# Two-bank PSUM copies and a first store in four DMAs, in a batched matrix product

## The chip, the cores and the metric

The kernel runs on one core of a Trainium2 chip. The metric is the device time of one execution in microseconds (us). Each kernel is executed several times, in rounds that alternate with the kernel before on the same chip, and most executions of a kernel agree within 0.3%. The span of the profile is about 2 us shorter than the time: it begins at the first instruction that the profiler shows. Executions over 1.5% above a kernel's fastest are called slow and are not used in ratios.

## The reference

```python
batch, m, k, n = 16, 512, 768, 1024
x: float32 (batch, k, m)      y: float32 (batch, k, n)
out = np.einsum('bkm,bkn->bmn', x, y)          # float32 (batch, m, n)
```

Inputs are 16 x 768 x (512 + 1,024) x 4 B = 75.5 MB, the output is 16 x 512 x 1,024 x 4 B = 33.55 MB. All of it has to cross the core's 16 DMA engines once.

## The kernel before

Each batch loads x and y in float32, casts them to bf16 on VectorE (DVE), multiplies on TensorE (PE) into PSUM, copies each 128x512 result to SBUF on ScalarE (ACT), and stores the whole 2 MB result in one DMA, four batches later. All DMAs are issued by one queue (SP), in program order.

```python
x_v = x.rearrange("b (p ko) m -> b p ko m", ko=KT)     # 12 KB contiguous per partition
y_v = y.rearrange("b (p ko) n -> b p ko n", ko=KT)     # 24 KB
o_v = out.rearrange("b (p mo) n -> b p mo n", mo=MT)   # 16 KB, MT = 4 blocks of 4 KB
...
psum = ctx.enter_context(tc.tile_pool(name="psum", bufs=8, space=bass.MemoryType.PSUM))
LAG = 4

def store(b):
    nc.sync.dma_start(o_v[b], o_tiles.pop(b)[:])

for b in range(B):
    ...
    load(xs[:], x_v[b], 1)                       # xs, ys: two buffers each
    ... load(ys[:, ks], y_v[b, :, ks], 1)        # one DMA; two halves for the last batch
    if b >= LAG:
        store(b - LAG)
    ... casts x_sb <- xs (one), y_sb <- ys (two halves)
    for h in range(halves):                      # 1, or 2 for the last batch
        for mo in range(MT):
            for nt in range(NT):                 # NT = 2, NF = 512
                if h == 0:
                    ps[mo, nt] = psum.tile([P, NF], FP32, name="ps")
                for kt in ...:
                    mm(ps[mo, nt], x_w, y_sb, kt, mo, nt)
                if h == halves - 1:
                    nc.scalar.copy(o_sb[:, mo, nt * NF:(nt + 1) * NF], ps[mo, nt][:])
for b in sorted(o_tiles):
    store(b)
```

## Time and profile before

| | before |
|---|---|
| time, median of the first 3 runs | 262.4 us (262.04 to 262.52) |
| span of the profiled execution | 260.5 us |
| DMA engines' time in packets of the one queue | 98.4% of the span |
| bytes | 109.06 MB in 49 DMAs |
| PE / DVE / ACT busy | 73% / 32% / 29% |

### The profile page before, as it was taken

The page shows a single profiled execution, that of the slowest core. Times are in us where ns is not written, and L with a number is a line of the kernel's source. Part 1 is how long each engine was busy: PE and PEld are TensorE (multiplying, and loading weights), DVE is VectorE, ACT ScalarE, POOL GpSimd, SP SyncE. Part 2 cuts the span into 40 slices and gives each one's busy share as a digit, 9 for nine tenths or more (in the row PEclk, how much of TensorE's full clock was granted, in tenths as well). Part 3 has the DMA queues.
Part 4 walks back from the last instruction along what each step waited for, and adds up shares of the span by engine and source line. Part 5 has one row for each costly group of instructions (what it writes and reads, how often), then busy time and mean ns, then how long its engine had stood idle before and what let it go on. Part 6 is the DMA issues. An engine that isn't in the chain of part 4 may idle for free.

```text
span 260.5 us, 1879 instructions
## 1 busy us (share of the span) xinstructions
PE 191.3 (73%) x768; PEld 89.3 (34%) x768; DVE 83.1 (32%) x48; ACT 76.4 (29%) x129; POOL 0.2 (0%) x4
## 2 busy tenths in 40 slices
PE   0049999897939959688496966969789395899600
PEld 0014555453513514334142432434335142355200
DVE  0271633525222252322524214252132522252000
ACT  1003444442421403324032330323314043141600
POOL 0000000000000000000000000000000000000000
PEclk9999999999985977979898896797979889799955
DMA  7999999999999999999999999999999999999994
GB/s 279 434 434 411 445 423 436 426 387 420 446 416 442 423 422 455 409 440 418 438 435 415 453 418 431 423 428 449 410 443 421 426 445 407 431 430 430 435 428 201
DMA packets 7065, 109.18 MB, mean 419 GB/s; under 512 B 784, under 2 KB 784, under 8 KB 784
## 3 DMA queue, kind: packets, MB, share of 16 engines
q1 hardware_dynamic: 7056, 109.06, 98.4%
q8 instruction: 6, 0.10, 0.1%
q14 instruction: 3, 0.02, 0.0%
HBM read 75.50 MB, written 33.55 MB: 419 GB/s over the span
## 4 chain that ended last, share of the span: by engine, by line
DMA 74%; DVE 11%; PE 8%; issue 0%; ACT 0%; SPq 0%; DVEq 0%
DMA ys<-in_y_dram 74%; DVE y_sb L78 11%; PE ps L56 8%; ACT o_sb L93 0%; SPq L50 0%; DVEq L78 0%
## 5 line engine op out<-in xcount | busy, mean ns | idle before, releaser
L56 PE MATMUL ps<-y_sb,x_sb 128*128 128x512 bf16 x768 | 191.3, 412 | 53.8 <-DVE y_sb L78 53.8
L56 PEld LDWEIGHTS <-x_sb 128*128 128x128 bf16 x768 | 89.3, 118 | 155.2 <-issue 45.9
L93 ACT COPY o_sb<-ps 128x512 f32<-128x512 f32 x128 | 75.1, 587 | 168.6 <-PE ps L56 168.2
L78 DVE CAST y_sb<-ys 128x3072 bf16<-128x3072 f32 x32 | 55.0, 1757 | 87.4 <-DMA ys<-in_y_dram 87.4
L75 DVE CAST x_sb<-xs 128x3072 bf16<-128x3072 f32 x16 | 28.2, 1760 | 66.6 <-DMA xs<-in_x_dram 60.4
L93 ACT ACT_TABLE_LOAD x1 | 1.3, 1283 | 0.7 <-PEq L110 0.7
L110 POOL MEMSET const-bfloat16-1.0<- 128x1 bf16 x1 | 0.1, 101 | 0.0
L110 POOL MEMSET const-uint8-127<- 128x1 uint8 x1 | 0.1, 101 | 0.0
L110 POOL MEMSET const-float32-0.0<- 128x1 f32 x1 | 0.1, 98 | 0.2 <-issue 0.2
L110 POOL MEMSET const-float32-1.0<- 128x1 f32 x1 | 0.1, 98 | 0.0
## 6 DMA issues: line engine op xcount, KB each, us to landing
ys<-in_y_dram SPq DMA_DIRECT2D x15, 3072.0 KB, 28.1
out_dram<-o_sb SPq DMA_DIRECT2D x16, 2048.0 KB, 32.6
xs<-in_x_dram SPq DMA_DIRECT2D x16, 1536.0 KB, 29.7
ys<-in_y_dram SPq DMA_DIRECT2D x2, 1536.0 KB, 26.1
```

Of the source, the lines that this page charges most:

```text
L56: nc.tensor.matmul(ps[:], x_w[:, kt, mo], y_sb[:, kt, nt * NF:(nt + 1) * NF], start=(kt == 0), stop=(kt == KT - 1))
L75: nc.vector.tensor_copy(x_sb[:], xs[:])
L78: nc.vector.tensor_copy(y_sb[:, ks], ys[:, ks])
L93: nc.scalar.copy(o_sb[:, mo, nt * NF:(nt + 1) * NF], ps[mo, nt][:])
L110: nc = _bacc.Bacc("TRN2", target_bir_lowering=False, num_devices=1)
```

## The change

The intent: fewer and longer copies out of PSUM (a copy takes two of the kernel's eight 128x512 result tiles at once; such a tile is called a bank here), which saves the fixed part of half of them, and a first store in pieces that could leave one by one. The diff, cut to its core (the helpers for loads and matmuls are also written out in place, with no effect on the program):

```diff
-    psum = ctx.enter_context(tc.tile_pool(name="psum", bufs=8, space=bass.MemoryType.PSUM))
+    psum = ctx.enter_context(tc.tile_pool(name="psum", bufs=4, space=bass.MemoryType.PSUM))
...
     def store(b):
-        nc.sync.dma_start(o_v[b], o_tiles.pop(b)[:])
+        o_sb = o_tiles.pop(b)
+        if b == 0:
+            for mo in range(MT):
+                nc.sync.dma_start(o_v[b, :, mo], o_sb[:, mo])
+            return
+        nc.sync.dma_start(o_v[b], o_sb[:])
...
+                    if h == 0:
+                        ps[mo] = psum.tile([P, NT, NF], FP32, name="ps")
                     for nt in range(NT):
-                        if h == 0:
-                            ps[mo, nt] = psum.tile([P, NF], FP32, name="ps")
...
-                        if h == halves - 1:
-                            nc.scalar.copy(o_sb[:, mo, nt * NF:(nt + 1) * NF], ps[mo, nt][:])
+                    if h == halves - 1:
+                        nc.scalar.copy(o_sb[:, mo].rearrange("p (t f) -> p t f", f=NF), ps[mo][:])
```

More of the change, by code (lines that the diff above doesn't have):

```diff
@@ L47 @@
     o_tiles = {}
-    def load(dst, src, rows):
-        nc.sync.dma_start(dst, src)
     def store(b):
-        nc.sync.dma_start(o_v[b], o_tiles.pop(b)[:])
-    def mm(ps, x_w, y_sb, kt, mo, nt):
-        nc.tensor.matmul(ps[:], x_w[:, kt, mo], y_sb[:, kt, nt * NF:(nt + 1) * NF],
-                         start=(kt == 0), stop=(kt == KT - 1))
+        o_sb = o_tiles.pop(b)
[4 more added lines that the diff above has]
+        nc.sync.dma_start(o_v[b], o_sb[:])
     with tc.manual_schedule():
@@ L64 @@
             halves = 2 if b == B - 1 else 1
-            load(xs[:], x_v[b], 1)
+            nc.sync.dma_start(xs[:], x_v[b])
             for h in range(halves):
                 ks = slice(h * KT // halves, (h + 1) * KT // halves)
-                load(ys[:, ks], y_v[b, :, ks], 1)
+                nc.sync.dma_start(ys[:, ks], y_v[b, :, ks])
             if b >= LAG:
@@ L86 @@
                 for mo in range(MT):
+                    if h == 0:
+                        ps[mo] = psum.tile([P, NT, NF], FP32, name="ps")
                     for nt in range(NT):
-                        if h == 0:
-                            ps[mo, nt] = psum.tile([P, NF], FP32, name="ps")
                         for kt in range(h * KT // halves, (h + 1) * KT // halves):
-                            mm(ps[mo, nt], x_w, y_sb, kt, mo, nt)
-                        if h == halves - 1:
-                            nc.scalar.copy(o_sb[:, mo, nt * NF:(nt + 1) * NF], ps[mo, nt][:])
+                            nc.tensor.matmul(
+                                ps[mo][:, nt], x_w[:, kt, mo],
+                                y_sb[:, kt, nt * NF:(nt + 1) * NF],
+                                start=(kt == 0), stop=(kt == KT - 1))
+                    if h == halves - 1:
+                        nc.scalar.copy(o_sb[:, mo].rearrange("p (t f) -> p t f", f=NF), ps[mo][:])
         for b in sorted(o_tiles):
```

## The prediction

> **What bounds the kernel now.** I read four views in this order: the page's busy shares and slices, the DMA queue totals, the stretches of time with each engine's work, and the DMA queue's own timeline. The page first:
>
> ```profile
> PE 191.3 (73%) x768; PEld 89.3 (34%) x768; DVE 83.1 (32%) x48; ACT 76.4 (29%) x129; POOL 0.2 (0%) x4
> ...
> DMA  7999999999999999999999999999999999999994
> GB/s 279 434 434 411 445 423 436 426 387 420 446 416 442 423 422 455 409 440 418 438 435 415 453 418 431 423 428 449 410 443 421 426 445 407 431 430 430 435 428 201
> ...
> q1 hardware_dynamic: 7056, 109.06, 98.4%
> ...
> HBM read 75.50 MB, written 33.55 MB: 419 GB/s over the span
> ...
> L56 PE MATMUL ps<-y_sb,x_sb 128*128 128x512 bf16 x768 | 191.3, 412 | 53.8 <-DVE y_sb L78 53.8
> ...
> L93 ACT COPY o_sb<-ps 128x512 f32<-128x512 f32 x128 | 75.1, 587 | 168.6 <-PE ps L56 168.2
> ```
>
> The reader is to see that no compute engine is above 73%, while the 16 DMA engines are busy 90% or more in 38 of 40 slices and queue q1's packets fill 98.4% of the engines' time. The bytes are the reference's: 75.5 MB of x and y in, 33.55 MB of output out, nothing read twice. Of the span of 260.5 us, the trace's packet records put the first data packet at 1.7 us and the last end at 259.3 us: 257.5 us from first to last, in which the packets fill 256.4 us per engine (98.4% of 260.5). Only about 1 us per engine is a gap. So the time is the sum of the packets' durations, plus about 3 us at the two ends.
>
> The chain of waits gives 74% to the y loads, 11% to the casts of y and 8% to matmuls. That is not three bounds in turn: a load waits for the cast that frees its buffer, but it is issued into a queue that is still long. The stretches show this best at the end (columns: PE, PEld, DVE, ACT, POOL busy us with counts; granted clock, DMA share, GB/s):
>
> ```profile
> 240.00:248.00 8.00, 5.03 (x24) 2.39 (x22) 0.00 (x0) 4.69 (x8) 0.00 (x0) 0.97 1.02 436
> 248.00:256.00 8.00, 0.00 (x0) 0.00 (x0) 0.00 (x0) 0.00 (x0) 0.00 (x0) 0.50 0.99 424
> 256.00:260.50 4.50, 0.00 (x0) 0.00 (x0) 0.00 (x0) 0.00 (x0) 0.00 (x0) 0.50 0.24 102
> ```
>
> All computing is over before 248 us, and the transfers still run at full share for another 8 us. The last store was issued at 245.7 us (chain: the last copy starts at 245.07 and takes 0.58) and its packets begin only at 252.2 us: it stood about 6.5 us behind older stores. **That 6.5 us is the slack** of the copy path at its most exposed point.
>
> **What the Trainium skill says.** (1) "DMA: Bandwidth & Descriptors", section "Where 436 GB/s comes from", gives 435 GB/s as the ceiling of the 16 ports and 425 as measured on large transfers. The trace agrees: while packets run, 109.06 MB in 256.0 us of data packets per engine is 426 GB/s, so there is about 2% to gain below the ceiling and no more. (2) The same page, "Why small descriptors are slow (HBM only)", says that each packet carries a fixed overhead of about 3 cycles. The trace shows a fixed part too, and I use its own size: median packets of 12,288, 16,384 and 24,576 B take 460, 611 and 912 ns, which is 0.0368 ns per byte plus 8 ns per packet. (3) "ScalarE: Activation LUTs", section "What ACT_TABLE_LOAD costs", gives 186 + 0.833 N ns for an instruction with immediate operands: 612 for N = 512, against 587 in this trace, so a little high here. (4) The DMA page's "Latency and other measured facts" reports that rows at a pitch of a large power of two can halve the rate, for pitches of 512 KiB and more; no row of this trace shows it, and the new store's pitch is 16 KiB.
>
> **The change, part by part.**
>
> PSUM copies. 128 copies of 512 columns become 64 of 1,024. With the page's slope, one takes 587 + 0.833 x 512 = 1,014 ns (estimate), so ACT is busy 64 x 1.014 = 64.9 us instead of 75.1: 10.2 us saved on an engine that is busy 29% and waits for PE in 168 us. Nothing of it is on the path. The copy of a pair's first half now waits for the second half's 6 matmuls, but PE keeps four pairs, the same 8 banks, and a pair comes round after 4 pairs of matmuls; the copy of 1.0 us is much shorter than three pairs' matmuls (36 x at least 0.216 = 7.8 us; where PE runs at full clock the timeline has a copy of 0.59 us and then 0.71 us of waiting for each 6 matmuls, 1.30 / 6 = 0.216), so PE should not wait for ACT. In the last batch each pair has 6 matmuls left in its second half, 6 x 0.216 = 1.3 us, more than 1.0, so copies keep up and the last ends 1.014 - 0.587 = 0.43 us later. Against 6.5 us of slack: 0 us on the end.
>
> First store. One DMA of 128 rows of 16 KB becomes four of 128 rows of 4 KB. Data packets go from 49 x 128 = 6,272 to 52 x 128 = 6,656, and completion packets (4 B, 9 ns) from 49 x 16 = 784 to 832, in all 7,056 to 7,488. A 4,096 B packet should take 8 + 4,096 x 0.0368 = 159 ns; four take 636 against 611, 25 ns more. Each engine carries 8 of the 128 rows: 8 x 25 = 200 ns, plus 3 x 9 = 27 ns. **Sum: +0.23 us**, and since the queue is the bound this is all on the path.
>
> Issue and waits. The store is issued by SP, in order with the loads:
>
> ```profile
> 31.72 0.33 SPq L50 DMA_DIRECT2D xs<-in_x_dram  x1
> 39.94 0.33 SPq L50 DMA_DIRECT2D ys<-in_y_dram  x1
> 40.32 0.42 SPq L53 DMA_DIRECT2D out_dram<-o_sb  x1
> 43.05 0.33 SPq L50 DMA_DIRECT2D xs<-in_x_dram  x1
> 52.01 0.33 SPq L50 DMA_DIRECT2D ys<-in_y_dram  x1
> 52.39 0.42 SPq L53 DMA_DIRECT2D out_dram<-o_sb  x1
> 54.05 0.33 SPq L50 DMA_DIRECT2D xs<-in_x_dram  x1
> 64.24 0.33 SPq L50 DMA_DIRECT2D ys<-in_y_dram  x1
> ```
>
> The first store's issue at 40.32 becomes four, 4 x about 0.46 = 1.9 us, done at 42.2, before the next load at 43.05 is released. The built program shows one more thing that the diff does not: a DMA may only be issued when the one eight before it, on the same of 8 completion semaphores, has landed. Three more DMAs shift this rotation. The x load of batch 6, issued at 54.05, now shares its semaphore with the y load of batch 4, which lands at 60.7 (chain of waits). So that issue moves from 54.05 to about 60.8, a **new wait of 6.7 us**. The queue then holds, behind that y load, the first store, x and y of batch 5 and the second store: 2.1 + 1.57 + 3.15 + 2.1 = 8.9 MB, at 426 GB/s some 21 us. The late load still enters 20 us before its turn, so 0 us. From batch 8 on the pairs of the rotation are as before.
>
> Sum: +0.2 us on 262.4 gives **262.6 us**.
>
> **Rivals.** (a) *The 4 KB rows at a 16 KB pitch are slow in HBM.* If 2.1 MB ran at half rate, the first store would take 9.8 us instead of 4.9: +4.9 us, about 267.3, just under 2% slower. For it speaks only point (4), at pitches 32 times larger; against it, the 16 KB rows too start at equal offsets on all engines and run at 26.8 GB/s per engine. I give it 5% in any strength. (b) *The late x load empties the queue.* It would be so if the backlog at 54 us were short; loads of y take a median of 28.1 us from issue to landing while their own bytes need 7.4, so some 20 us of backlog is the rule. If I have it wrong by all of the 6.7 us: 269. I give 1%. (c) *The copy was holding PE and a faster ACT frees it*, so that casts and loads come earlier. PE waits in the list of waits only for casts of y (53.8 us), never for ACT, and earlier loads only lengthen the queue: 262.4. (d) *Smaller packets fill the gaps between engines or smooth the shared ports.* There is about 1 us of gap in all, and one store of 16 can touch a small part of it: -0.3 us at best.
>
> **Range and chances.** The three runs before spread over 0.5 us. With +0.2 from the packets, and another execution's spread of about 0.3% either way, the range is 261.7 to 263.8, wider above because (a) and (b) only lengthen. A gain of 2% would need 5.2 us, which the bytes do not allow: 1%. A loss of 2% needs (a) or (b) near full strength: 1.5%. The rest, 97.5%, is within 2%.
>
> **What would show each step.** The page of the changed kernel should have q1 at 7,488 packets, 109.06 MB and about 98.4%; "under 8 KB" rising by 512 + 48 = 560 to 1,344; 64 ACT copies of 128x1024 at about 1,014 ns and ACT near 66 us busy; the list of waits still without a wait of PE for ACT; four store issues from 40.3 to about 42.2 us and an x load at about 60.8 in place of 54.05; the y load's period (112.06 to 127.86 in the queue's timeline, 15.8 us) unchanged; the last store issued at about 246 and landing about 13.5 us later. Wrong would be: 4,096 B packets far above 159 ns (then a is right), DMA slices below 9 between 60 and 80 us (then b), or a gap in the transfers near 246 us (then the slack was not there).

## The result, and the profile after

| | before | after |
|---|---|---|
| time, median of 4 runs each | 262.25 us (262.04 to 262.52) | 262.74 us (262.61 to 262.90) |
| ratio | | 1.0017, 95% interval 1.0002 to 1.0032 |
| span of the profiled execution | 260.5 us | 260.8 us |

A ratio is the mean time of one kernel's fast runs over that of the other's fast runs of the same rounds, so it is not quite the ratio of the medians. Here it is +0.45 us (0.0017 x 262.25): within 2%, slower by a hair.

The page of the changed kernel; its lines answer to the first fence of the prediction:

```profile
PE 191.2 (73%) x768; PEld 89.4 (34%) x768; DVE 83.1 (32%) x48; ACT 66.2 (25%) x65; POOL 0.2 (0%) x4
...
DMA  7999999999999999999999999999999999999994
GB/s 279 434 434 418 452 419 432 422 364 425 432 420 441 420 428 435 422 437 427 428 443 415 445 412 438 432 425 439 425 435 422 424 444 418 425 438 427 427 435 206
...
q1 hardware_dynamic: 7488, 109.06, 98.5%
...
L93 ACT COPY o_sb<-ps 128x1024 f32<-128x1024 f32 x64 | 64.9, 1014 | 179.2 <-PE ps L88 179.2
```

ACT has lost 10.2 us of work, exactly its 64 copies of 1,014 ns against 128 of 587, and has gained about as much waiting (179.2 us for PE instead of 168.2). The DMA row is as full as before. The largest difference in the GB/s row is its ninth value, 364 against 387 (the sixteenth, 435 against 455, is nearly as large, so one value proves little): that slice (52 to 59 us) holds the end of the y load of batch 4 and the beginning of the first store.

The queue's timeline of the changed kernel (start, duration, then the DMA and how many are merged in the line):

```profile
39.98 0.33 SPq L67 DMA_DIRECT2D ys<-in_y_dram  x1
40.36 1.85 SPq L54 DMA_DIRECT2D out_dram<-o_sb  x4
42.77 0.34 SPq L64 DMA_DIRECT2D xs<-in_x_dram  x1
51.74 0.34 SPq L67 DMA_DIRECT2D ys<-in_y_dram  x1
52.17 0.38 SPq L57 DMA_DIRECT2D out_dram<-o_sb  x1
60.56 0.33 SPq L64 DMA_DIRECT2D xs<-in_x_dram  x1
64.05 0.33 SPq L67 DMA_DIRECT2D ys<-in_y_dram  x1
```

The four issues end at 42.2 us and the next load goes out in time, at 42.77. The x load of batch 6 goes out at 60.56 instead of 54.05. In the list of the queue's waits this is a line of its own (waiter, what it waited for, us in total, times, longest). The kernel before issues all loads from one line and cannot show it, but the list of run e3 below, which has the store whole and its loads on lines of their own, has no such line:

```profile
SPq L64 <- DMA ys<-in_y_dram: 7.9, 1, 7.9
```

The end, in stretches, with the same columns as in the prediction:

```profile
240.00:248.00 8.00, 5.08 (x24) 2.45 (x22) 0.00 (x0) 4.05 (x4) 0.00 (x0) 0.96 1.00 426
248.00:256.00 8.00, 0.00 (x0) 0.00 (x0) 0.00 (x0) 0.00 (x0) 0.00 (x0) 0.50 1.02 436
256.00:260.80 4.80, 0.00 (x0) 0.00 (x0) 0.00 (x0) 0.00 (x0) 0.00 (x0) 0.50 0.29 123
```

As before, no compute engine works after 248 us while the transfers run on.

### The profile page after: what moved, and what is told of

Same layout as the page of the kernel before. It is cut to its first block, busy times and chain, and to the rows that moved or that the text cites. A ratio compares the mean times of both kernels' runs of the same rounds, so it can differ in the third digit from the quotient of the medians.

```text
span 260.8 us, 1822 instructions
## 1 busy us (share of the span) xinstructions
PE 191.2 (73%) x768; PEld 89.4 (34%) x768; DVE 83.1 (32%) x48; ACT 66.2 (25%) x65; POOL 0.2 (0%) x4
## 2 busy tenths in 40 slices
DMA packets 7498, 109.18 MB, mean 419 GB/s; under 512 B 833, under 2 KB 833, under 8 KB 1345
## 3 DMA queue, kind: packets, MB, share of 16 engines
q1 hardware_dynamic: 7488, 109.06, 98.5%
## 4 chain that ended last, share of the span: by engine, by line
DMA 74%; DVE 11%; PE 8%; ACT 0%; issue 0%; SPq 0%; DVEq 0%
DMA ys<-in_y_dram 74%; DVE y_sb L75 11%; PE ps L88 8%; ACT o_sb L93 0%; SPq L64 0%; DVEq L75 0%
## 5 line engine op out<-in xcount | busy, mean ns | idle before, releaser
L93 ACT COPY o_sb<-ps 128x1024 f32<-128x1024 f32 x64 | 64.9, 1014 | 179.2 <-PE ps L88 179.2
```

Of the source, the lines that this page charges most:

```text
L93: nc.scalar.copy(o_sb[:, mo].rearrange("p (t f) -> p t f", f=NF), ps[mo][:])
```

## The experiments

The theory at the start: the queue is the bound, the PSUM part is worth nothing, and the four-way store costs its extra packets. The rivals: the copies do matter (at the end above all), 4 KB writes are slow in HBM, or the shifted rotation of the eight completion semaphores (explained in the prediction) lets the transfers down. Twelve kernels ran, all with correct results.

### The two parts, each alone

**e1** is the changed kernel again, with five rounds.

> Theory (only the packets of the first store cost anything): +0.23 us over the kernel before, so a ratio near 1.0009, q1 again at 7,488 packets. Rival (the late x load or slow 4 KB writes cost the 0.45 us that was measured first): ratio 1.0017 or above again.

Measured: 262.79 us against 262.01, ratio 1.0026 (1.0011 to 1.0040).

**e2** is the kernel before with the four-way first store alone.

```diff
-        nc.sync.dma_start(o_v[b], o_tiles.pop(b)[:])
+        o_sb = o_tiles.pop(b)
+        if b == 0:
+            for mo in range(MT):
+                nc.sync.dma_start(o_v[b, :, mo], o_sb[:, mo])
+            return
+        nc.sync.dma_start(o_v[b], o_sb[:])
```

> The four-way first store alone, single-bank copies kept. Theory: the same +0.23 us as the whole change, 4,096 B packets at 159 ns, x load of batch 6 issued near 60.6 us. Rival (the PSUM part matters): less than the whole change's difference.

Measured: 262.64 us, ratio 1.0022 (1.0009 to 1.0035).

**e3** is the changed kernel without the `if b == 0` branch: the PSUM part alone.

> Two-bank copies alone, store kept whole. Theory: 0.0 us, ACT 66 us busy instead of 76, x load of batch 6 back at about 54 us, q1 at 7,056 packets. Rival (the copies give or take time): a ratio clear of 1.

Measured: 261.98 us, ratio 1.0001 (0.9988 to 1.0013); ACT busy 66.2 us, q1 at 7,056 packets.

The three ran on one chip in the same rounds. The whole difference is the store's, and the PSUM part is worth nothing, as predicted. But the size is about 0.6 us (0.0022 and 0.0026 of 262.01), where 0.23 was predicted, and the lower end of e1's interval, 0.29 us, is above that. So the sign and the part are settled and the size is not.

### Which property of the four-way store costs: its rows or its DMAs?

The change makes rows of 4 KB and also makes four DMAs of one. To see either, it was applied to all 16 stores of the kernel before.

**e5** pads the output tile in SBUF, so that each store is still one DMA but breaks into 4 KB rows.

```diff
-            o_sb = o_pool.tile([P, MT, N], FP32, name="o_sb")
+            o_sb = o_pool.tile([P, MT, N + 16], FP32, name="o_sb")[:, :, :N]
```

(Here and in e11 the store's line only drops its `[:]`.)

> Kernel before with a padded output tile: all 16 stores in rows of 4 KB, one DMA each, so no change in the number of DMAs. Theory (8 ns per packet): 16 x 8 x 25 ns = +3.2 us, about 265.5, median packet 159 ns. Rival (small writes slow in HBM): clearly more than 3.2 us.

Measured: 263.52 us against 262.20, ratio 1.0053 (1.0038 to 1.0068). Its queue line:

```profile
q1 hardware_dynamic: 13200, 109.06, 99.1%
```

The packets are the predicted ones: median 159 ns in the trace's records, and 99.1% of 261.8 us is 259.4 us per engine against 256.4 before, +3.0 us. Yet the time rose by only 1.3 us. The records show how this goes together: the 16 engines have 17 or more packets under way at once for 42.7 us of this span, and for 23.3 us of the span before, so a packet's record can begin before its predecessor's has ended. Spread over the 16 engines, this overlap is 2.9 us each here and 1.6 us before, so about 1.4 of the 3.0 us are counted twice. **Adding up packet records counts part of the time twice.** What a packet added, if all of the loss is put down to packets, is 1.32 us / (24 x 16 = 384 extra packets per engine) = 3.4 ns (2.6 to 4.6 by the interval of the ratio), not 8. The Trainium skill, "DMA: Bandwidth & Descriptors", section "Why small descriptors are slow (HBM only)", speaks of about 3 cycles per packet; with the 850 MHz that the same page gives for the fabric this would be 3.5 ns (an estimate from the page), which lies within what this run shows.

**e6** makes all 16 stores as the change makes the first.

```diff
-        nc.sync.dma_start(o_v[b], o_tiles.pop(b)[:])
+        o_sb = o_tiles.pop(b)
+        for mo in range(MT):
+            nc.sync.dma_start(o_v[b, :, mo], o_sb[:, mo])
```

> Kernel before with all 16 stores as the change makes the first: four DMAs of 4 KB rows at a 16 KB pitch. Theory: 3.2 us of packets + 0.4 us of completions = +3.6 us, about 265.9. Rival of the pitch: more than the padded single DMA's by over 1 us; if 4 KB rows at this pitch ran at half rate it would be +78 us. Rival of the rotation's waits: DMA slices below 9.

Measured: 269.34 us, ratio 1.0278 (1.0260 to 1.0297): +5.8 us over e5, although the rows are the same. This is 0.36 us for each store (5.82 / 16), where the extra completion packets account for 0.03. The rates and DMA shares of its page, and below them the rates of e5:

```profile
DMA  7999999999999999999999999999999999999993
GB/s 294 418 436 427 438 427 423 436 353 436 426 404 443 363 446 425 415 440 365 445 418 425 440 364 446 411 434 434 376 443 409 441 408 394 436 413 413 419 417 145
```

```profile
GB/s 300 422 426 426 438 431 436 424 342 431 433 411 439 423 436 434 416 434 411 437 436 421 438 406 444 422 429 436 409 446 412 433 439 409 437 415 417 423 423 237
```

The reader is to see two things. The engines are busy 90% or more in every slice but the first and the last, so the queue did not run dry. And every fifth slice of e6's rates falls to 353 to 394 GB/s, where e5, with the same rows, has only one such value, the ninth (342). Five slices are 33 us, two batches. In the packet records these are the y loads of batches 4, 6, 8, 10, 12 and 14: in each, 20 to 31 of the 128 packets take over 1,000 ns, 1,247 to 1,324 ns at their median, where 912 is the rule; no other y load of e6 has more than 5 such packets. The first of them begin 0.6 to 3.0 us before the first packet of the store behind, so they are not simply loads that run beside stores. The kernel before has such a stretch once, at 56 us (the 387 in its own GB/s row, 31 slow packets), with no store split and no load late. About 3 us of e6's loss lie in these stretches (the packets of y take 948 ns in the mean instead of 921, and each engine has 120 of them). Another 1.4 us appear in the last 3% of the bytes, where the engines end further apart: 16 packets are under way until 4.8 us before the last one ends, against 3.4 us in the kernel before. Slow writes at the 16 KB pitch are not the reason: the 4 KB packets keep their 159 ns.

**e7** breaks all stores into rows of 1 KB, one DMA each, by a tile of 16 padded pieces.

```diff
-            o_sb = o_pool.tile([P, MT, N], FP32, name="o_sb")
+            o_pad = o_pool.tile([P, MT, 4, N // 4 + 8], FP32, name="o_sb")
+            o_sb = o_pad[:, :, :, :N // 4]
```

(Copies and stores are written for this shape.)

> Kernel before with all stores in rows of 1 KB, one DMA each. Theory (a fixed 8 ns per packet): a packet takes 8 + 37.7 = 46 ns, 16 of them 731 ns against 611, 120 x 8 x 16 = +15.4 us, about 277.8. Rival (the cost of small packets grows faster than a fixed part): packets well above 46 ns, over 280 us.

Measured: 281.49 us median, of which two of four runs are slow, the profiled one among them; the fast ones give 1.0655 (1.0613 to 1.0697), +17.2 us. The 1,024 B packets take 46 ns, as expected, but the agreement of the total with the expected +15.4 is not to be trusted: e5 shows that packet sums overstate, and in this (slow) profile SP's own issuing has become 7% of the chain that ended last. The run says that 1 KB rows are dear, and not by which mechanism.

### The rotation of semaphores: two tests that failed as tests

**e4** and **e8** were to press the rotation harder with packets left at 16 KB, by splitting each store by partitions.

```diff
-        nc.sync.dma_start(o_v[b], o_tiles.pop(b)[:])
+        o_sb = o_tiles.pop(b)
+        for p in range(0, P, P // 4):            # e8: P // 8
+            nc.sync.dma_start(o_v[b, p:p + P // 4], o_sb[p:p + P // 4])
```

> Kernel before with every store as four DMAs of 32 partitions, rows still 16 KB: the rotation of the 8 completion semaphores bites in every batch (a store's later parts must wait for landings of the same or the last batch's loads), packets keep their size. Theory (waits hidden by the backlog): 16 x 3 x 9 ns of completion packets = +0.4 us, 262.7. Rival (the rotation's waits empty the queue): several us more, DMA slices below 9.

> Kernel before with every store as eight DMAs of 16 partitions, rows of 16 KB. Only 8 DMAs may be in flight, so the backlog falls to about one batch. Theory (backlog still over the waits): 16 x 7 x 9 ns = +1.0 us, 263.4. Rival (the queue runs dry in each batch): more than 2 us over that, with DMA slices below 9.

Measured: e4 279.46 us at the median of six runs, two of them slow, and 1.0638 (1.0606 to 1.0669) from the fast ones; e8 325.08 us, 1.2412 (1.2373 to 1.2451). Both expectations were far off, and the edit is to blame. Late stretches of e4 and then of e8, in which the only transfers left are stores:

```profile
258.00:270.00 12.00, 0.00 (x0) 0.00 (x0) 0.00 (x0) 0.00 (x0) 0.00 (x0) 0.57 0.96 262
```

```profile
280.00:310.00 30.00, 4.29 (x20) 2.04 (x18) 0.00 (x0) 4.52 (x8) 0.00 (x0) 0.65 0.93 210
```

The engines are busy (0.96 and 0.93) and move 262 and 210 GB/s, where whole stores move 436 (the changed kernel from 248 to 256 us, above). Over the whole runs, the same 16 KB packets take 694 and 889 ns in the mean instead of 612. The number of DMAs is not enough to explain this, since e6's four over all 128 partitions move 413 to 419 GB/s in its last full slices. So a store of 32 or 16 partitions is slow in itself here, and these runs say nothing clean about the rotation. They do warn of something else: the share of busy DMA engines does not tell whether they move at full rate.

### The copies at the end

**e9** and **e10** are the changed kernel with 4 and 10 useless copies ahead of the very last one; the result is unchanged.

```diff
+                        if b == B - 1 and mo == MT - 1:
+                            for _ in range(4):          # e10: 10
+                                nc.scalar.copy(o_sb[:, mo - 1]..., ps[mo - 1][:])
                         nc.scalar.copy(o_sb[:, mo]..., ps[mo][:])
```

> Changed kernel with 4 useless copies of 128x1024 (about 1.01 us each) ahead of the very last copy, the result unchanged. Theory (6 us of slack behind older stores): the last store is issued about 4 us later, near 250.2, and the time stays within 0.3 us of the changed kernel's. Rival (copies at the end are on the path): +4 us.

> The same with 10 useless copies, about 10 us. Theory: the slack is used up; the last store goes out near 256.1, and alone needs 4.9 us of bytes and about 2.7 us of latency, so it lands near 263.7: about +3.8 us over the changed kernel. Rival (copies on the path): +10 us; rival (more slack than thought): 0.

Measured: e9 262.73 us, ratio 1.0030 (1.0014 to 1.0047), the changed kernel's time; e10 265.04 us, ratio 1.0119 (1.0091 to 1.0148), 2.3 us more. The stretches of e10:

```profile
248.00:256.00 8.00, 0.00 (x0) 0.00 (x0) 0.00 (x0) 7.50 (x8) 0.00 (x0) 0.58 0.54 229
256.00:260.50 4.50, 0.00 (x0) 0.00 (x0) 0.00 (x0) 0.00 (x0) 0.00 (x0) 0.50 0.96 408
```

Now the transfers do pause (0.54) while ACT works (7.50 of 8 us). Its last copy ends at 255.7 us, and the store lands 6.3 us later; the changed kernel's last store lands at 246.1 + 13.5 = 259.6. So a copy that ended at 259.6 - 6.3 = 253.3 would just be free: the slack is 7.2 us. The 0.43 us by which the long copy ends later are far inside it. My +3.8 for e10 was too much because a store alone lands in 6.3 us, and not in the 7.6 that I took.

### One DMA against four, at the first store and elsewhere

After e6 I held that the change's cost came from the slow stretch near 56 us, where the first store begins. Two last kernels tested that, on the kernel before.

**e11** makes only the first store in 4 KB rows, but as one DMA; this also undoes the shift of the semaphores.

```diff
-            o_sb = o_pool.tile([P, MT, N], FP32, name="o_sb")
+            o_all = o_pool.tile([P, MT * (N + 16)], FP32, name="o_sb")
+            w = N + 16 if b == 0 else N
+            o_sb = o_all[:, :MT * w].rearrange("p (m n) -> p m n", m=MT)[:, :, :N]
```

> Kernel before with only the first store in rows of 4 KB, but as one DMA: the packets of the change without its extra DMAs and without the shift of the semaphores. Theory (the rows cost the time, not the late x load): the transfers fall behind by about 0.4 us between 46 and 72 us, as in the changed kernel (0.2 to 0.5 there), q1 at 7,440 packets, x load of batch 6 back at about 54 us. Rival (the late x load or the four issues cost the 0.4 us): no step, ratio 1.000.

Measured: 262.13 us against 262.20, ratio 0.9996 (0.9984 to 1.0009), q1 at 7,440 packets, the x load of batch 6 back at 54.71 us.

**e12** splits the store of batch 5 into four in place of batch 0 (`if b == 5` in e2).

> Kernel before with the store of batch 5 instead of batch 0 as four DMAs of 4 KB rows. Theory (the rows cost about 0.1 us a store in the steady state, the rest came from the stretch near 56 us where the first store begins): +0.1 us, ratio about 1.0004, no new step between 46 and 72 us. Rival (four DMAs cost 0.4 us wherever they stand): a step of 0.4 us between 120 and 145 us, ratio 1.0015 or more.

Measured: 263.51 us, ratio 1.0048 (1.0035 to 1.0062): +1.3 us, where 0.1 was expected. Its GB/s row, of which the 24th value (151 to 157 us) is to be compared with the 418 of the kernel before:

```profile
GB/s 264 433 427 427 457 409 433 420 397 425 441 415 440 425 431 435 418 442 415 434 413 424 435 371 437 429 429 439 425 432 425 431 442 421 427 434 427 427 435 160
```

Where transfers fall behind can be worked out from the packet records: the time by which a share of the bytes (17, 27, 47, 62 and 97%) has moved, less the same for the kernel before. One profiled execution each; the kernel before reaches these shares at the times in the head, and differences of 0.3 us at the last packet are within the spread of executions. The profiled execution of e2 (262.32 us) was the fastest of its five, that of e12 (264.13 us) the slowest of its five.

```
                        45.8    71.9   122.7   160.7   249.7 us   last packet
changed kernel         -0.04    0.35    0.42    0.45    0.39          0.02
e1 (the same again)    -0.08    0.45    0.32    0.32    0.29          0.30
e2 store alone          0.03    0.32    0.21    0.20    0.12         -0.18
e3 PSUM alone           0.06    0.03   -0.11   -0.13   -0.20         -0.04
e11 one DMA, first      0.11    0.34    0.24    0.22    0.15         -0.25
e12 four DMAs, batch 5  0.14    0.15    0.29    1.32    1.16          1.55
e5 4 KB rows, all      -0.18    0.33    0.60    0.88    1.52          1.29
e6 four DMAs, all      -0.12    0.41    2.17    3.29    5.34          6.73
```

The four kernels with a 4 KB first store (the changed kernel, e1, e2, e11) lose 0.2 to 0.5 us between 46 and 72 us and keep it from there to within 0.2 us, while e3 loses nothing. e12 loses nothing there and 1.0 us between 123 and 161: its records show slow packets late in the y load of batch 10 (mean of the load 1,001 ns), one batch after the split store, again with no gap in the DMA row. In e5, where this store has the same rows in one DMA, that load keeps 914 ns. So my theory of the special first store fell: e11, with the same rows at the same place, costs nothing that five rounds can tell from zero, and four DMAs elsewhere cost more than at the first store, not less.

What stays: **the form of four DMAs costs, the rows hardly do.** e2 against e11 is 0.0026 of 262, some 0.7 us, in separate rounds on two chips, and rests on the run times alone: in the table both fall behind by 0.2 to 0.3 us at the first store and end alike. e6 against e5 is 5.8 us in the same rounds. Why four DMAs make later y packets slow is open. Four DMAs always come with a shift of the rotation, and so with a later load (in e12 the x load of batch 10 goes out at 124.50 us instead of 118.94, the y load at 129.38 instead of 127.86), and no run has the one without the other. No version came out clearly faster than the kernel before; the PSUM part alone equals it.

## Why the prediction was right

The time of 262.74 us lies by the predicted 262.6 and inside 261.7 to 263.8. By its own steps:

- **The bound.** Right. Taking 10.2 us from ACT left the time at a ratio of 1.0001 (e3). But "only about 1 us per engine is a gap" is misread: it is what is left when the overlap of the records (1.6 us per engine) is set against the idle time (2.7 us).
- **The copies.** Right to the nanosecond: 1,014 ns, 64.9 us, and PE never waits for ACT. The slack at the end was taken as 6.5 us and measures 7.2 (e9, e10).
- **The queue's counts.** Right: 7,488 packets, packets of 4,096 B at a median of 159 ns, and 1,345 below 8 KB against 1,344 predicted (the one more is of another queue, q14).
- **The issues and the rotation.** Right as to when: done at 42.2 us, the x load at 60.56 where 60.8 was said, 6.5 us late instead of 6.7. That it enters the backlog in time and that no engine goes idle is right too.
- **"Sum: +0.23 us".** Right in sign, and of the right order, but both terms are mis-sized. The rows' term of 0.20 us is too large: 24 packets x 3.4 ns (e5) are 0.08 us, because packet records overlap and their sum is not time. The term for three more DMAs, 27 ns of completion packets, is too small: about 0.36 us per store in e6 against e5. The two errors offset each other in part, so that the time lands close to 262.6 is in part luck (the base of 262.4 was also a little above the median of 262.25 in the end). The total of 0.45 to 0.8 us in the runs with the four-way first store is nearer to the second term than to the first.
- **Rival (a), slow 4 KB writes.** Refuted: their packets take 159 ns at the median in every run, whether four DMAs write them (e6) or one (e5). Point (4) was also weaker support than it was made: the page has 207 of 214 GB/s at a pitch of 512 KiB, and about half only from 4 MiB.
- **Rival (b), the late load empties the queue.** Refuted as it was put, since the DMA row is full. But e12 and e6 show a form of loss that it did not think of: no gap, only slower packets. Whether the late load has a part in it is open.
- **Rivals (c) and (d).** No gain from either: e3 is 1.0001, and no kernel with the four-way store is faster.

## What to carry to other kernels

Where the transfers fill the span, sort each part of a change by whether it touches packets, the backlog or nothing, and put the parts on the chip alone: here the large-looking part is worth zero and the small one all of the difference. In a kernel like this, keep a store one DMA over all 128 partitions unless an early piece is needed by someone: here its row length of 4 or 16 KB matters far less than the number of DMAs or a split by partitions. And read the GB/s row beside the DMA row, because engines can be busy all the time and still be slow (e8: 0.93 busy at 210 GB/s).

## What the Trainium skill lacked or had wrong

- "DMA: Bandwidth & Descriptors", on the cost of small descriptors: its fixed 3 cycles per packet fit the time that e5 lost (3.4 ns per packet), but not the packet records of the trace, whose fixed part is 8 ns. No page says that the packet records of a profile overlap and must not be added up (2.9 us per engine in e5).
- No page has the cost of cutting a 2 MB store into four of 512 KB behind a full queue: 0.36 us per store when all are cut (e6 against e5), 1.3 us for one cut store in mid-stream (e12), as slower packets of later loads and not as idle engines.
- No page has the limit of eight DMAs in flight that the built program sets through its completion semaphores, by which three more DMAs moved another load from 54.05 to 60.56 us.
- "ScalarE: Activation LUTs" gives 186 + 0.833 N ns: the slope holds, (1,014 - 587) / 512 = 0.834 ns, and the fixed part of these copies from PSUM to SBUF is 160 ns.
